# Reloading split weights through GpSimd's queue straight into the operand tiles of a 2048-frame encoder trunk

## The chip, the cores and the metric

The kernel runs on one core of one Trainium2 chip. The metric is the device time of one execution in microseconds. Three runs of the kernel before gave 2957.13, 2957.32 and 2959.49 us; the median is 2957.32 us.

## The reference

The reference is one layer of a streaming encoder for 2048 frames of width 1024, all in float32. A normed input goes through one projection (26 column blocks of 128). Its first columns feed a gated short convolution, the others an RWKV-7 recurrence of 8 heads that runs along time. Both results go through an output projection, then come a gated feed-forward block with a width-3 convolution (up to 5632 columns, down from 2816), and an embedding gated by a last projection. In outline:

```python
h = rms_norm(x, mix_norm_g);  z = h @ w_in
y = concat(short_conv_mixer(z[..., :1536]), rwkv7_mixer(z[..., 1536:]))
x = x + y @ w_out
u = causal_dwconv(rms_norm(x, ffn_norm_g) @ ffn_w_up, ffn_conv_w) + ffn_conv_b
x = x + (silu(gate) * val) @ ffn_w_down          # gate, val: the halves of u
e = rms_norm(p @ ple_w_proj, ple_norm_g)
x = x + sigmoid(rms_norm(x, ple_gate_norm_g) @ ple_w_gate) * e
return rms_norm(x, final_norm_g)
```

## The kernel before

Time is cut into four groups of 512 frames, and a product writes a 128 x 512 block of output columns by frames. Every dense product is done as three TensorE products of float32r operands: the weights and the activations are each split into a rounded part (hi) and the remainder (lo), and `mm3` adds hi·hi, hi·lo and lo·hi in one PSUM bank. One half is the unit in which weights arrive: a tile `whl` of 128 x 1024 whose left 512 columns are hi and whose right 512 are lo. It serves 12 products of 512 columns. A group needs 220 halves: 52 for the input projection and 168 for the rest (16 for `w_out`, 88 for `w_up`, 44 for `w_down`, 4 for `w_proj`, 16 for `w_gate`).

The program first runs the input projection for all four groups (`all_in`), then the dense rest for all four groups (`dense_rest`). Beside these products goes the recurrence in 16 units of 128 frames (`rwkv_unit`). A driver lets it take a step each time a product yields, so that its many small products stand between the dense ones on TensorE. TensorE's order is that of the code, since every matmul is pinned. The order on the other engines is set by a scheduler that places each instruction by estimated times. Each engine and each queue then runs its list strictly in that order.

`half` (L156 to L174) makes a half ready. The first time that a weight block is needed (the first group of the input projection and the first group of the dense rest), SP loads 256 KB of the original weights into a tile `raw`, ScalarE rounds it into hi (L153), GpSimd subtracts to get lo (L154), and SP writes the pair to a tensor `keep` in HBM (L172). Each later group takes the pair from there: SP loads 512 KB into a 128 x 1024 `raw` tile (L162), and ScalarE casts it to float32r into the operand tile (L163). There are two `raw` tiles (`WRAW`) and four operand tiles (`WHL`). A load therefore waits until the cast before the last has read its `raw` tile, and a cast waits until TensorE is done with the half four places ahead.

SP's queue carries, beside the weights: the frames of x, the mixer's results y and the embedding e (L204), the rows of x that are added after the output projection (L396, pinned in order, each into one of ten `x2` tiles), and the recurrence's loads (L562 to L567, L774, L789, L802, L809). GpSimd does, beside the lo parts of first weights: the lo part of the feed-forward activations (`lo<-th`, L154), the halo columns of the convolutions (`zb<-u_last` and `u_last<-zb`, L257 and L258), and steps of the recurrence: `s` (L613), `gd` (L573), `pb` and `pbl` (L717 to L723), two memsets of `lm` (L786), four copies `tt<-dt` (L820), and the power `gr` (L589). ScalarE evacuates and activates, and copies the state and the token operands of the recurrence.

Of the kernel before, what the change touches and what calls it, by code (L numbers as in the profile page):

```python
# [9 lines left out]
F32 = mybir.dt.float32  # L10
# [6 lines left out]
P = 128  # L17
# [11 lines left out]
RATE = 1.0  # L29
SLOW = 0.85  # L30
WRAW = 2
WHL = 4
NBUF = 6
NLD = 3
ACT = 32
# [27 lines left out]
def tile_trunk(  # L63
# [18 lines left out]
    nc = tc.nc  # L82
# [69 lines left out]
    def residual(raw, hi, lo):  # L152
        nc.scalar.copy(hi, raw)  # L153
        nc.gpsimd.tensor_tensor(out=lo, in0=raw, in1=hi.bitcast(F32), op=ALU.subtract)  # L154

    def half(pools, src, name, key):  # L156
        t = pools["w"].tile([P, 1024], F32R, tag="whl", name=f"whl{name}", bufs=WHL)
        hi, lo = t[:, 0:512], t[:, 512:1024]
        raw = pools["w"].tile([P, 1024], F32, tag="raw", name=f"raw{name}", bufs=WRAW)
        with tc.high_priority():  # L160
            if key in kept:
                nc.sync.dma_start(out=raw, in_=kept[key])  # L162
                nc.scalar.copy(t, raw)  # L163
                return hi, lo
            first = raw[:, 0:512]
            if len(src.shape) == 3:
                nc.sync.dma_start(out=first.rearrange("p (j c) -> p j c", j=2), in_=src)
            else:
                nc.sync.dma_start(out=first, in_=src)
            residual(first, hi, lo)  # L170
        keep = dram.tile([P, 1024], F32, tag=f"k{name}", name=f"k{name}")
        nc.sync.dma_start(out=keep, in_=t.bitcast(F32))  # L172
        kept[key] = keep
        return hi, lo  # L174

    kept = {}

    def weight(pools, src, name):
        return [
            half(pools, src[:, 512 * c : 512 * c + 512], f"{name}_{c}", f"{name}_{c}")  # L180
            for c in range(2)
        ]

    def quad(pools, src, mp, name):
        cols = slice(256 * mp, 256 * mp + 256)
        return [half(pools, src[:, :, cols].rearrange("j p c -> p j c"), name, name)]
# [746 lines left out]
    pools, rp = {}, {}  # L933
# [139 lines left out]
```

## Time and profile before

| | |
|---|---|
| median of three runs | 2957.32 us |
| the profiled execution | 2957.25 us |
| its span, first to last instruction | 2955.5 us |
| TensorE (PE) busy | 2784.5 us, 94% |
| weight loads into TensorE (PEld) | 2232.1 us, 76% |
| VectorE (DVE) busy | 1888.8 us, 64% |
| ScalarE (ACT) busy | 1611.2 us, 55% |
| GpSimd (POOL) busy | 763.3 us, 26% |
| DMA | 630 MB, 213 GB/s over the span |
| granted TensorE clock, mean | 0.977 |

The span is the time that the engines' rows cover; 1.75 us of the execution lie outside it. Busy shares are means over stages that differ: the input projection of the first group ends at about 196 us, that of the others at about 700 us; the dense rest of the first group goes to about 1330 us, the others follow to the end. The last unit of the recurrence ends at about 2614 us.

### The profile page before, as it was taken

Reading aid. Unit: us, or ns where it says so; the run is one execution under the profiler, and the core shown is the slowest. Engines: PE = TensorE matmul, PEld = TensorE weight load, DVE = VectorE, ACT = ScalarE, POOL = GpSimd, SP = SyncE. Lnnn points to the kernel's source line nnn. Section 1 sums busy time; section 2 is a strip of 40 time slices with the busy share of each in tenths; the row PEclk is TensorE's granted clock in tenths of the full one; section 3 lists DMA queues with packets and bytes.
Section 4 is the critical chain, followed back from the end, with each engine's and each line's share of the span. In section 5 each row is a group of like instructions: output and inputs, shape, how many; then the busy total and the mean of one; then the engine's idle time right before and its main releaser. Section 6 shows DMA issues by size and latency. Waiting matters only on the chain.

```text
span 2955.5 us, 43233 instructions
## 1 busy us (share of the span) xinstructions
PE 2784.5 (94%) x15464; PEld 2232.1 (76%) x15464; DVE 1888.8 (64%) x3039; ACT 1611.2 (55%) x2381; POOL 763.3 (26%) x1040
## 2 busy tenths in 40 slices
PE   8899999999888999988999999889999998999997
PEld 6677777778676767766788887767888876788885
DVE  4575655657586767696676677757675764544346
ACT  4345565544453434355755556667565565755555
POOL 4521010203455555550211121102111210211110
PEclk9999999999999999999999999999999999999998
DMA  8776766577776676767665655666565557666664
GB/s 295 262 262 220 225 209 220 191 228 241 239 245 237 231 251 217 249 228 258 194 193 170 188 182 176 219 204 204 177 196 170 187 184 244 203 195 197 192 195 150
DMA packets 285810, 630.02 MB, mean 213 GB/s; under 512 B 60186, under 2 KB 113690, under 8 KB 285596
## 3 DMA queue, kind: packets, MB, share of 16 engines
q1 hardware_dynamic: 229184, 578.91, 60.5%
q10 hardware_dynamic: 56412, 48.36, 5.0%
q8 instruction: 122, 2.00, 0.3%
q14 instruction: 92, 0.75, 0.1%
HBM read 467.77 MB, written 159.38 MB: 212 GB/s over the span
## 4 chain that ended last, share of the span: by engine, by line
PE 44%; DMA 20%; DVE 14%; ACT 10%; issue 8%; POOL 3%; ACTq 1%; SPq 0%; DVEq 0%; POOLq 0%
PE ps_mm L86 28%; PE ps_d L86 10%; DMA rawu<-ku 3%; DMA rawin<-kin 2%; DMA rawu<-in_w_up 2%; DMA rawin<-in_w_in 2%; DVE uf L416 2%; DMA rawo<-ko 2%; DMA x<-in_xT 2%; DVE pd L793 1%; ACT whlu L163 1%; ACT whlin L163 1%; PE o_ps L86 1%; DVE xs L797 1%; DMA dt<-xd 1%
## 5 line engine op out<-in xcount | busy, mean ns | idle before, releaser
L86 PE MATMUL ps_mm<-hi,whlu 128*128 128x512 f32 x2816 | 915.5, 399 | 11.1 <-POOL whlu L154 8.1
L86 PEld LDWEIGHTS ps_mm<-hi,whlu 128*128 128x128 f32 x2816 | 535.2, 190 | 132.7 <-POOL whlu L154 11.2
L86 PE MATMUL ps_mm<-hi,whlin 128*128 128x512 f32 x1664 | 545.4, 402 | 15.0 <-ACT whlin L153 7.0
L86 PE MATMUL ps_mm<-lo,whlu 128*128 128x512 f32 x1408 | 555.2, 394 | 1.5 <-DVE lo L216 1.5
L86 PE MATMUL ps_d<-hi,whld 128*128 128x512 f32 x1408 | 453.9, 395 | 8.2 <-DVE x L456 3.6
L163 ACT CAST whlu<-rawu 128x1024 fp32r<-128x1024 f32 x264 | 277.2, 1051 | 283.0 <-DMA rawu<-ku 194.3
L416 DVE SCALAR_TENSOR_TENSOR uf<-zb,vec,uf 128x512 f32<-128x512 f32 x352 | 291.0, 829 | 206.5 <-ACT uf L411 196.3
L86 PEld LDWEIGHTS ps_mm<-hi,whlin 128*128 128x128 f32 x1664 | 317.7, 191 | 89.8 <-ACT whlin L153 8.0
L86 PE MATMUL ps_mm<-lo,whlin 128*128 128x512 f32 x832 | 330.0, 397 | 1.3 <-DVE lo L216 1.3
L86 PEld LDWEIGHTS ps_d<-hi,whld 128*128 128x128 f32 x1408 | 264.9, 188 | 69.7 <-DVE x L456 6.0
L86 PEld LDWEIGHTS ps_mm<-lo,whlu 128*128 128x128 f32 x1408 | 268.4, 191 | 56.8 <-DVE lo L216 2.5
L86 PE MATMUL ps_d<-lo,whld 128*128 128x512 f32 x704 | 275.0, 391 | 0.0
L163 ACT CAST whlin<-rawin 128x1024 fp32r<-128x1024 f32 x156 | 163.2, 1047 | 160.2 <-DMA rawin<-kin 78.2
L256 DVE TENSOR_TENSOR zb<-ps_mm,rstd 128x512 f32<-128x512 f32 x216 | 148.1, 685 | 102.3 <-PE ps_mm L86 97.3
L456 DVE TENSOR_TENSOR x<-ps_d,x 128x512 f32<-128x512 f32 x192 | 130.9, 686 | 124.8 <-PE ps_d L86 124.1
L163 ACT CAST whld<-rawd 128x1024 fp32r<-128x1024 f32 x132 | 138.5, 1051 | 125.4 <-DMA rawd<-kd 61.6
L86 PE MATMUL ps_mm<-hi,whlo 128*128 128x512 f32 x512 | 168.4, 404 | 23.3 <-ACT whlo L163 11.4
L86 PEld LDWEIGHTS ps_mm<-lo,whlin 128*128 128x128 f32 x832 | 159.3, 191 | 36.3 <-DVE lo L216 4.3
L154 POOL TENSOR_TENSOR lo<-th,hi 128x512 fp32r<-128x512 f32 x88 | 116.7, 1327 | 219.0 <-ACT hi L153 218.4
L411 ACT ACTIVATE uf<-zb,vec 128x512 f32<-128x512 f32 x176 | 142.8, 813 | 44.2 <-DVE zb L256 42.4
L86 PE MATMUL ps_mm<-hi,whlg 128*128 128x512 f32 x512 | 165.7, 399 | 0.2 <-ACT whlg L163 0.2
L86 PEld LDWEIGHTS ps_d<-lo,whld 128*128 128x128 f32 x704 | 132.6, 188 | 25.8
(204 smaller groups left out, 4341.8 us busy)
## 6 DMA issues: line engine op xcount, KB each, us to landing
rawu<-ku SPq DMA_DIRECT2D x264, 512.0 KB, 4.2
rawin<-kin SPq DMA_DIRECT2D x156, 512.0 KB, 4.2
rawd<-kd SPq DMA_DIRECT2D x132, 512.0 KB, 4.1
ku<-whlu SPq DMA_DIRECT2D x88, 512.0 KB, 4.4
kin<-whlin SPq DMA_DIRECT2D x52, 512.0 KB, 4.9
rawo<-ko SPq DMA_DIRECT2D x48, 512.0 KB, 4.5
rawg<-kg SPq DMA_DIRECT2D x48, 512.0 KB, 4.1
rawu<-in_w_up SPq DMA_DIRECT2D x88, 256.0 KB, 3.5
```

The source lines that it names most:

```text
L86: return pin(nc.tensor.matmul(*args, **kw))
L154: nc.gpsimd.tensor_tensor(out=lo, in0=raw, in1=hi.bitcast(F32), op=ALU.subtract)
L163: nc.scalar.copy(t, raw)
L256: nc.vector.tensor_tensor(out=zb[:, 2 : G + 2], in0=ps, in1=rstd, op=ALU.mult)
L411: nc.scalar.activation(u, zb[:, 2 : G + 2], AF.Identity, bias=v("ffn_conv_b", n), scale=v("ffn_conv_w", 88 + n),)
L416: nc.vector.scalar_tensor_tensor(out=u, in0=zb[:, d : d + G], scalar=v("ffn_conv_w", 44 * d + n), in1=u, op0=ALU.mult, op1=ALU.add,)
L456: nc.vector.tensor_tensor(out=x2[m], in0=ps, in1=x2[m], op=ALU.add)
L793: tt(out=pd[:, :, :, 0:n], in0=xs[:, :, None, 0:n].broadcast_to([P, 8, 2, n]), in1=lm[:, None, i : i + 2, 0:n].broadcast_to([P, 8, 2, n]), ...
L797: nc.vector.tensor_reduce(out=xs[:, :, i : i + 2], in_=pd[:, :, :, 0:n], op=ALU.add, axis=mybir.AxisListType.X,)
```

## The change

Where a half has been kept, its load no longer goes from SP's queue into a `raw` tile with a cast by ScalarE behind it. GpSimd's queue issues one DMA from `keep` (float32) to the operand tile (float32r), and the DMA converts. The `raw` tiles are only needed for first loads and shrink from 1024 to 512 columns, and the operand tiles go from four to five.

```diff
-WHL = 4
+WHL = 5
...
     def half(pools, src, name, key):
         t = pools["w"].tile([P, 1024], F32R, tag="whl", name=f"whl{name}", bufs=WHL)
         hi, lo = t[:, 0:512], t[:, 512:1024]
-        raw = pools["w"].tile([P, 1024], F32, tag="raw", name=f"raw{name}", bufs=WRAW)
+        if key in kept:
+            with tc.high_priority():
+                nc.gpsimd.dma_start(out=t, in_=kept[key])
+            return hi, lo
+        first = pools["w"].tile([P, 512], F32, tag="raw", name=f"raw{name}", bufs=WRAW)
         with tc.high_priority():
-            if key in kept:
-                nc.sync.dma_start(out=raw, in_=kept[key])
-                nc.scalar.copy(t, raw)
-                return hi, lo
-            first = raw[:, 0:512]
```

ScalarE's list where the scores of the last unit of the recurrence are made. `whld` and `whlu` are halves of the down and up weights, `tok` the recurrence's token operand; before:

```order
L428 ACTIVATE th<-uf 128x512 [waits Pool_49]
L722 CAST pbh_21677<-pb_21674 128x512 [waits Pool_49]
L163 CAST whld_2_21786<-rawd_2_21787 128x1024 [waits DMAHW5_49,PE_49]
L163 CAST whld_2_21790<-rawd_2_21791 128x1024 [waits DMAHW6_49,PE_49]
L153 CAST hi<-th 128x512 [waits DVE_49]
L756 COPY tok_0_21749<-ps_k 128x512 [waits PE_49]
L163 CAST whld_3_21931<-rawd_3_21932 128x1024 [waits DMAHW7_49,PE_49,Activation_49]
L163 CAST whld_3_21935<-rawd_3_21936 128x1024 [waits DMAHW0_49,PE_49,Activation_49]
L756 COPY tok_1_21809<-ps_k 128x512 [waits PE_49]
```

The same place now:

```order
L427 ACTIVATE th<-uf 128x512 [waits Pool_49]
L721 CAST pbh_20797<-pb_20794 128x512 [waits Pool_49]
L153 CAST hi<-th 128x512 [waits DVE_49]
L755 COPY tok_0_20861<-ps_k 128x512 [waits PE_49]
L755 COPY tok_1_20917<-ps_k 128x512 [waits PE_49]
```

The casts, each with a wait for a DMA and for TensorE, no longer stand between the recurrence's copies.

GpSimd's list a little later in the same unit, around the memsets of `lm`; before:

```order
L723 TENSOR_TENSOR pbl_21678<-pb_21674,pbh_21677 128x512 [waits Activation_49]
L154 TENSOR_TENSOR lo<-th,hi 128x512 [waits Activation_49]
L786 MEMSET lm_21839 128x32 [waits DMAHW3_49,DMAHW2_49,DMAHW4_49,DMAHW1_49,DVE_49]
L787 MEMSET lm_21839 128x16
L257 COPY zb<-u_last 128x2 [waits Pool_49]
L258 COPY u_last<-zb 128x2 [waits DVE_49]
```

Now:

```order
L161 DMA whlu_0_21153<-ku_0_10807 128x1024 [waits DMASW7_49,PE_49]
L161 DMA whlu_1_21155<-ku_1_10814 128x1024 [waits DMASW0_49,PE_49]
L161 DMA whlu_0_21190<-ku_0_10854 128x1024 [waits DMASW1_49,PE_49]
L256 COPY zb<-u_last 128x2 [waits Pool_49]
L257 COPY u_last<-zb 128x2 [waits DVE_49]
L785 MEMSET lm_20947 128x32 [waits DMAHW6_49,DMAHW5_49,DMAHW7_49,DMAHW0_49,DVE_49]
L786 MEMSET lm_20947 128x16
L161 DMA whlu_1_21192<-ku_1_10861 128x1024 [waits DMASW2_49,PE_49]
L161 DMA whlu_0_21235<-ku_0_10909 128x1024 [waits DMASW3_49,PE_49]
```

Weight loads that wait for TensorE now stand ahead of and behind GpSimd's steps that wait for VectorE or for the recurrence's DMAs.

SP's list at the start of the last group's output projection (`rawo` are its weights, `x_3_n` the rows of x); before:

```order
L162 DMA rawo_0_23444<-ko_0_6966 128x1024
L162 DMA rawo_1_23448<-ko_1_6973 128x1024
L396 DMA x_3_2_23347<-in_xT 128x512
L396 DMA x_3_3_23390<-in_xT 128x512
L396 DMA x_3_4_23433<-in_xT 128x512
L396 DMA x_3_5_23476<-in_xT 128x512
L162 DMA rawo_0_23487<-ko_0_7015 128x1024
L162 DMA rawo_1_23491<-ko_1_7022 128x1024
```

Now:

```order
L395 DMA x_3_1_22277<-in_xT 128x512
L203 DMA p<-in_pT 128x512 x2
L395 DMA x_3_2_22351<-in_xT 128x512
L395 DMA x_3_3_22390<-in_xT 128x512
L395 DMA x_3_4_22429<-in_xT 128x512
L395 DMA x_3_5_22468<-in_xT 128x512
L395 DMA x_3_6_22507<-in_xT 128x512
```

The weight loads and the rows of x no longer share a list.

## Rows read from the trace of the kernel before

**Rows 1.** The page's part 1: busy us, share of the span, instructions.

```profile
PE 2784.5 (94%) x15464; PEld 2232.1 (76%) x15464; DVE 1888.8 (64%) x3039; ACT 1611.2 (55%) x2381; POOL 763.3 (26%) x1040
```

**Rows 2.** Busy time of each engine in stretches, granted clock, DMA share, GB/s.

```profile
196.00:700.00 504.00, 491.21 (x3016) 396.66 (x3016) 297.32 (x516) 283.55 (x412) 71.85 (x160) 0.99 0.68 217
1330.00:2895.00 1565.00, 1510.38 (x8284) 1218.32 (x8282) 978.46 (x1627) 945.78 (x1298) 261.50 (x444) 0.99 0.62 196
...
1325.00:1395.00 70.00, 62.96 (x259) 49.48 (x259) 51.93 (x89) 37.10 (x47) 7.46 (x11) 0.95 0.81 260
1890.00:1960.00 70.00, 63.36 (x273) 50.26 (x273) 51.56 (x91) 39.37 (x50) 4.55 (x9) 0.95 0.75 243
2437.00:2507.00 70.00, 61.30 (x255) 47.94 (x255) 36.67 (x55) 41.26 (x52) 4.82 (x4) 0.98 0.75 245
```

**Rows 3.** PE's waits from 1330 to 2895 us: waiter, releaser, us, times, longest.

```profile
PE ps_mm L86 <- ACT whlo L163: 11.4, 8, 3.0
PE ps_mm L86 <- DVE x L397: 8.1, 2, 4.4
...
PE ps_e L86 <- ACT hi L153: 3.6, 1, 3.6
...
PE ps_o L86 <- ACT tok L756: 2.3, 2, 1.3
...
PE ps_e L86 <- ACT e L371: 2.2, 4, 1.0
PE ps_mm L86 <- ACT hi L215: 1.7, 2, 1.0
```

**Rows 4.** PE's waits from 196 to 700 us.

```profile
PE x_ps L86 <- ACT gm L589: 4.9, 3, 2.3
PE ps_b L86 <- ACT tok L756: 2.3, 1, 2.3
PE ps_mm L86 <- ACT whlin L163: 1.9, 1, 1.9
```

**Rows 5.** Chain of waits, 2440 to 2500 us: start, us, what.

```profile
2443.61 5.34 DMA rawo<-ko
2449.04 1.06 ACT whlo L163
```

**Rows 6.** SP's queue in order of time, 2440 to 2500 us.

```profile
2456.64 20.50 SPq L162 DMA_DIRECT2D rawo<-ko  x7
2478.11 4.54 SPq L396 DMA_DIRECT2D x<-in_xT  x4
```

**Rows 7.** The casts of line 163 alone: ScalarE's busy time and count in stretches.

```profile
196.00:700.00 504.00, 159.03 (x152) 0.99 0.68 217
1330.00:2895.00 1565.00, 517.05 (x493) 0.99 0.62 196
```

**Rows 8.** Chain of waits where the recurrence is over: 16 halves on TensorE.

```profile
2614.77 43.52 PE ps_mm L86 x192
```

**Rows 9.** Line 162, SP's loads: issue ns (min/median/max), and us to landing.

```profile
L162 SPq DMA_DIRECT2D rawu<-ku x264: 319/320/692, 1385.1 to 2841.7; - x132
...
DMA to landing us min/median/max: 3.0/4.2/8.4
```

**Rows 10.** GpSimd's groups, whole span: busy us, mean ns, idle before, releasers.

```profile
L820 POOL COPY tt<-dt 32x256 f32<-32x256 f32 x64 | 27.6, 432 | 193.7 <-DMA dt<-xd 191.5
L589 POOL TENSOR_TENSOR gr<-var,neg_h 128x8 f32<-128x8 f32 x16 | 26.3, 1643 | 123.6 <-DVE var L589 122.0 <-DMA rawu<-in_w_up 1.6
...
L786 POOL MEMSET lm<- 128x32 f32 x16 | 2.6, 160 | 97.7 <-DVE lm L785 85.4 <-ACT whlin L163 7.0 <-DMA p<-in_pT 5.3
```

**Rows 11.** VectorE's copies, whole span.

```profile
L589 DVE COPY w_t<-w_ps 128x256 f32<-128x256 f32 x32 | 13.5, 420 | 13.3 <-PE w_ps L86 13.1
L589 DVE COPY tt<-x_ps 32x256 f32<-32x256 f32 x32 | 13.3, 414 | 24.4 <-PE x_ps L86 24.2
```

**Rows 12.** SP's queue on the 16 DMA engines: packets, MB, share of the span.

```profile
q1 hardware_dynamic: 229184, 578.91, 60.5%
```

## The prediction

> **What bounds the kernel now.** I read the page's busy shares first, then the busy time by stretches, then TensorE's waits in those stretches, then the chain of waits where they are longest. TensorE is busy 2784.5 of 2955.5 us [rows 1], so nothing that shortens another engine's work can give back more than its idle time and its slow clock. The change acts only where kept halves are loaded. The casts of line 163 show where that is: 152 of them between 196 and 700 us, 493 between 1330 and 2895 us [rows 7]. In these two stretches of 2069 us TensorE is idle 12.8 + 54.6 = 67.4 us, at a granted clock of 0.99 [rows 2]. The rest of the idle time lies in the first loads, the start and the tail, where neither path of a kept half runs.
>
> Within the two stretches the idle time is not spread evenly. Where all is steady, 16 halves take 43.52 us [rows 8], so TensorE uses up a half in 2.72 us. In the first 70 us of each later group's output projection it is idle 7.0, 6.6 and 8.7 us and has a clock of 0.95, 0.95 and 0.98 [rows 2]. There the chain runs through the weights' supply: a load of 5.34 us, a cast of 1.06 us, the next load [rows 5]. Two raw tiles give two halves per such round of 6.4 us, 3.2 us for one, slower than TensorE's 2.72. The queue shows the same pace: seven loads issued in 20.50 us, 2.93 us each. Then four loads of x hold SP for 4.54 us more, with weights behind them [rows 6]. The waits name it too: products of the output projection stood 11.4 us for the cast of `whlo`, and 8.1 us for rows of x that share SP's queue [rows 3]; 1.9 us went to a cast of the input weights [rows 4].
>
> **The change, part by part.**
>
> *ScalarE's casts go.* 645 casts, 676 us of ScalarE in these stretches, or 1.05 us each [rows 7]. That is beside TensorE's work, except where TensorE waits for the result. The direct waits for a cast are 11.4 + 1.9 = 13.3 us [rows 3, 4]; with the supply no longer cut into rounds of load and cast I count them gone: **-13.3 us**. ScalarE's other results that TensorE waits for, behind casts in its list, are `gm` 4.9, `tok` 2.3 and 2.3, `hi` 3.6 and 1.7, `e` 2.2 us [rows 3, 4], together 17.0 us. The least gain is none, if their inputs were late by themselves, and the most is 17.0. The two lists of ScalarE show casts directly ahead of `tok`, but not each wait had one ahead, so I take half: **-8.5 us**.
>
> *SP's queue loses its weight loads.* The loads of x then stand behind no load that waits for a raw tile. Of the 8.1 us [rows 3] I take half, since those loads also wait for a free `x2` tile: **-4 us**.
>
> *Clock.* In the three output-projection stretches a clock of 0.95, 0.95 and 0.98 over 70 us [rows 2] costs (0.05 + 0.05 + 0.02) x 70 = 8.4 us. The lower level is 1.2 GHz, half of 2.4, and idle time goes with it in these rows. About half of the idle time there goes, so I take half: **-4 us**.
>
> *GpSimd's queue gains 645 DMAs in these stretches.* No row of before shows a DMA from that queue, nor one that converts. For the issue the nearest rows are SP's 0.32 us for the same 512 KB [rows 9] below, and GpSimd's costliest short instruction, `gr` with 1.64 us [rows 10], above. I take the middle, 0.98 us. Then 645 issues are 632 us, beside 72 + 262 = 333 us of GpSimd's own work in 2069 us [rows 2]: 47% of its time, at the upper end 67%. GpSimd does not become the bound. For the landing, SP's loads show 3.0 to 8.4 us with a median of 4.2 [rows 9]; a converting one could be shorter than the median only by what queues saved, so I keep 4.2 and hold 8.4 as the upper end.
>
> *Five tiles.* A load waits until TensorE has finished the half five places ahead and has the time of four halves, 4 x 2.72 = 10.9 us. It needs 0.98 + 4.2 = 5.2 us, which leaves a cover of 5.7 us. At the upper ends it needs 1.64 + 8.4 = 10.0 us, with 0.8 us left. So the supply holds as long as GpSimd comes to the load in time. Without the fifth tile the cover would be 3.0 us.
>
> *What is queued behind the new wait.* Each load waits for TensorE at GpSimd's head, and behind it stand halo copies, `lo<-th`, and the recurrence's `s`, `lm`, `tt` and `gr`; VectorE and then TensorE wait for those. There is a load every 2.72 us or more, so an instruction that comes at a random time waits up to 1.4 us on average if GpSimd always stands at a load, and about 0.3 us (0.98 us by a share of 0.31) if loads never wait. I take 1.2 us. Four such places in each unit of the recurrence, 12 units in these stretches (three quarters of the 16 counted by `gr` [rows 10]), are 58 us of delay in that chain. TensorE has dense products to do meanwhile, so most of it is covered. I charge a quarter, a choice between none and all: **+14 us**.
>
> The Trainium skill has a rule against this change (SBUF — State Buffer, section "SBUF: two separate sides"): while VectorE runs a copy in its two-port mode, GpSimd cannot write descriptors, and a DMA issued from its queue starves. What the trace shows of VectorE's copies are 64 in the whole span, 26.8 us, and all read a PSUM tile (`w_ps`, `x_ps`) [rows 11]; the rule speaks of copies from SBUF to SBUF. If the rule held for these too, 48 copies of 0.42 us in the kept stretches would add 20 us to GpSimd in pieces far below the cover of 5.7 us, so by the rule as by the rows the sum stays the same.
>
> *First loads.* They keep their path; a narrower raw tile changes none of their instructions, and the fifth tile can help where ScalarE waited for a free one. I count zero.
>
> **Sum.** -13.3 - 8.5 - 4 - 4 + 14 = -15.8 us. The profiled execution took 2957.25 us, of which 1.75 lie outside the span, and the median of the runs is 2957.32, the same within 0.1. So 2957.25 - 15.8 = **2941 us**.
>
> **The rivals.**
>
> *GpSimd blocked (slower).* GpSimd's own waits in before: 193.7 us ahead of `tt<-dt`, 123.6 ahead of `gr`, 97.7 ahead of `lm` [rows 10], over 16 units 12.1, 7.7 and 6.1 us each. They cost nothing there, since nothing stood behind. Now weight loads stand behind. Where such a wait is longer than the cover of 5.7 us, TensorE runs dry: 6.4 + 2.0 + 0.4 = 8.8 us a unit, 106 us over 12 units if the waits stay as long. Against it: in before GpSimd came early to these places because it had nothing else to do; with loads paced by TensorE it comes later, and the scheduler places a memset by when it expects it. Half is 53 us, less the 13 us of direct waits that would still go: 2957 + 40 = **2997 us**. It decides from a wait above 5.7 us with a load next in the list.
>
> *Converting DMAs move data slowly (slower).* SP's queue moved 578.91 MB in 60.5% of the span [rows 12], 0.324 MB per us of all engines. 645 kept halves of 0.524 MB are 338 MB, 1043 us, half of the 2069 us; the DMA share there is 0.62 to 0.68 [rows 2]. If converting doubled the time the engines would need 1.14 times the stretch: 0.14 x 2069 = 290 us, **3247 us**. It decides from about 1.7 times the plain duration. Nothing in the rows speaks for it, since none shows a conversion.
>
> *Hidden anyway (no change).* The 67 us of idle time are mostly the recurrence's own; the weights' waits go, and GpSimd's new delays put back as much: within 5.9 us of 2957 (0.2%, about what a measurement of this kernel tells from no change).
>
> *The larger gain.* If all 17.0 us of waits on ScalarE, all 8.1 for x and all 8.4 of clock go, with GpSimd's delays covered: 13.3 + 17.0 + 8.1 + 8.4 = 47 us, **2910 us**.
>
> **How the numbers follow.** The forecast (2918 to 2951) has 0.40, the larger gain 0.13, hidden anyway 0.14, GpSimd blocked 0.25, slow conversion 0.08. Faster by over 0.2%: 0.53; within: 0.14; slower: 0.33. The forecast's own range is 2918 to 2951 us. With both signs held, the range goes from 2900 us, a little below the larger gain, to 3010 us, a little above half the price of a blocked GpSimd; what is left out is its full price, the slow conversion, and little below.
>
> **What would show it.** Right: no cast of line 163 on ScalarE, its busy time near 1611 - 690 = 920 us; TensorE's waits for `whlo` gone and the output-projection stretches nearly without idle time; GpSimd's busy time or its queue up by about 0.3 to 1.6 us a load; loads landing in 4 to 8 us. Wrong: TensorE's new waits end with a DMA into `whl`, and GpSimd stood at `tt`, `gr` or `lm` ahead of it (blocked), or DMA shares in the kept stretches go toward 1 (slow conversion).

## The result and the profile after

The changed kernel takes 2916.45 us (median of three, 2914.06 to 2920.32) against 2957.32 us: ratio 0.9861, 95% interval 0.9839 to 0.9884, or 41 us less. The forecast was 2941. The sign was right, the size was less than half of what came, and the forecast's own range (2918 to 2951) was missed at its lower end; the wide range held it. The profiled execution took 2920.32 us with a span of 2918.5 us.

Part 1 of the page after, as [rows 1]:

```profile
PE 2771.0 (95%) x15464; PEld 2231.7 (76%) x15464; DVE 1894.1 (65%) x3039; ACT 962.9 (33%) x1721; POOL 1109.2 (38%) x1700
```

ScalarE has 660 instructions and 648 us less. GpSimd has 660 instructions and 346 us more: the issue of each load stands there as busy time.

Busy time by stretches after (columns as in [rows 2]). The first two are the stretches of the kept halves, the other three the first 70 us of each later group's output projection, each begun 9 to 12 us ahead of its first product as in [rows 2]:

```profile
196.00:686.00 490.00, 482.62 (x3013) 390.25 (x3011) 301.12 (x521) 134.66 (x261) 151.87 (x313) 1.00 0.73 223
1315.00:2857.00 1542.00, 1505.29 (x8279) 1220.94 (x8277) 980.86 (x1624) 460.16 (x803) 518.38 (x936) 0.99 0.66 198
1309.50:1379.50 70.00, 64.04 (x300) 51.18 (x298) 50.90 (x93) 20.51 (x31) 17.62 (x32) 0.98 0.84 265
1873.50:1943.50 70.00, 64.36 (x302) 51.87 (x301) 48.04 (x88) 20.19 (x31) 14.79 (x30) 0.98 0.84 259
2421.30:2491.30 70.00, 67.97 (x289) 54.83 (x288) 35.55 (x53) 21.59 (x33) 16.40 (x28) 0.98 0.83 270
```

The two stretches are 504 - 490 = 14 and 1565 - 1542 = 23 us shorter, so all of the difference of the two profiled executions (36.9 us) lies where kept halves are loaded. TensorE's idle time in them falls from 67.4 [rows 2] to 7.4 + 36.7 = 44.1 us, by 23.3. That is not the whole of the 37: its busy time falls too, from 2001.6 [rows 2] to 482.6 + 1505.3 = 1987.9 us, by 13.7 for the same work. In the three 70 us stretches it is idle 6.0, 5.6 and 2.0 us at a clock of 0.98, where it was 7.0, 6.6 and 8.7 at 0.95, 0.95 and 0.98. The same 70 us now hold 300, 302 and 289 products instead of 259, 273 and 255, the dense ones and the recurrence's small ones counted together.

TensorE's waits after, 1315 to 2857 us, answering to [rows 3]:

```profile
PE ps_g L86 <- DVE suv L653: 7.6, 3, 3.3
PE ps_mm L86 <- DVE lo L215: 6.0, 4, 2.4
PE ps_mm L86 <- DVE x L396: 5.9, 2, 3.2
...
PE ps_mm L86 <- DMA whlo<-ko: 2.0, 1, 2.0
PE ps_e L86 <- ACT tok L755: 1.4, 1, 1.4
...
PE ps_d L86 <- DMA whld<-kd: 1.0, 2, 0.6
...
PE ps_e L86 <- ACT e L370: 0.6, 1, 0.6
PE ps_mm L86 <- ACT hi L214: 0.5, 1, 0.5
```

The same from 196 to 686 us, answering to [rows 4]:

```profile
PE ps_mm L86 <- DMA whlin<-kin: 2.4, 4, 1.2
...
PE ps_b L86 <- ACT tok L755: 1.2, 1, 1.2
...
PE x_ps L86 <- ACT gm L588: 0.3, 1, 0.3
```

No product waits for a cast. What is left of ScalarE as a releaser is small, and the head of the list is now VectorE. Over all rows of the two stretches, the waits that name ScalarE fall from 33.6 to 5.2 us, and 5.4 us of waits for loads come up. The waits that name VectorE stay: 32.6 us before, 32.4 after.

GpSimd after: two of the groups of loads, and the groups that answer to [rows 10]:

```profile
L161 POOL DMA_DIRECT2D whlu<-ku x264 | 141.8, 537 | 422.9 <-PE ps_mm L86 278.3 <-PE ps_d L86 97.9 <-PE ps_e L86 17.7
...
L819 POOL COPY tt<-dt 32x256 f32<-32x256 f32 x64 | 29.3, 458 | 68.3 <-DMA dt<-xd 65.9
L588 POOL TENSOR_TENSOR gr<-var,neg_h 128x8 f32<-128x8 f32 x16 | 27.5, 1719 | 20.0 <-DVE var L588 19.6
...
L161 POOL DMA_DIRECT2D whlo<-ko x48 | 25.7, 538 | 77.4 <-PE ps_mm L86 76.8 <-issue 0.6
...
L785 POOL MEMSET lm<- 128x32 f32 x16 | 2.5, 159 | 39.1 <-DVE lm L784 39.0
```

Issues of line 161 (ns, min/median/max) and landing, answering to [rows 9], and the queue's line, answering to [rows 12]:

```profile
L161 POOL DMA_DIRECT2D whlu<-ku x264: 527/528/612, 1360.1 to 2807.1; - x132
L161 POOL DMA_DIRECT2D whlin<-kin x156: 527/529/735, 187.1 to 689.8; - x156
...
DMA to landing us min/median/max: 3.4/4.5/11.0
```

```profile
q0 software_dynamic: 95040, 346.07, 39.4%
```

VectorE's waits show that ScalarE's list is lighter; the first of these fences is the kernel before, the second the one after (waiter, releaser, us, times, longest):

```profile
DVE uf L416 <- ACT uf L411: 196.3, 107, 5.5
```

```profile
DVE uf L415 <- ACT uf L410: 100.8, 91, 6.1
```

VectorE waited half as long for ScalarE's `uf`, while its busy time stayed (1888.8, 1894.1). ScalarE used to be the later of the two; now it is idle ahead of `uf` and waits for VectorE's `zb`. TensorE's waits that name VectorE did not fall with this (32.6, 32.4). The group of `uf` on ScalarE, before and after:

```profile
L411 ACT ACTIVATE uf<-zb,vec 128x512 f32<-128x512 f32 x176 | 142.8, 813 | 44.2 <-DVE zb L256 42.4
```

```profile
L410 ACT ACTIVATE uf<-zb,vec 128x512 f32<-128x512 f32 x176 | 143.1, 815 | 526.8 <-DVE zb L255 481.3 <-issue 44.1
```

### The profile page after: what moved, and what is told of

The parts are those of the page before. It is cut to its first block, busy times and chain, and to the rows that moved or that the text cites. A ratio compares the mean times of both kernels' runs of the same rounds, so it can differ in the third digit from the quotient of the medians.

```text
span 2918.5 us, 42094 instructions
## 1 busy us (share of the span) xinstructions
PE 2771.0 (95%) x15464; PEld 2231.7 (76%) x15464; DVE 1894.1 (65%) x3039; ACT 962.9 (33%) x1721; POOL 1109.2 (38%) x1700
## 3 DMA queue, kind: packets, MB, share of 16 engines
q0 software_dynamic: 95040, 346.07, 39.4%
## 4 chain that ended last, share of the span: by engine, by line
PE 49%; DVE 20%; DMA 16%; ACT 5%; issue 5%; POOL 3%; ACTq 1%; SPq 0%; DVEq 0%; POOLq 0%
PE ps_mm L86 33%; PE ps_d L86 11%; DVE uf L415 3%; DVE pd L792 3%; DMA rawu<-in_w_up 2%; DMA lm<-ld 2%; DVE xs L796 2%; DMA rawin<-in_w_in 2%; DMA x<-in_xT 1%; DVE zb L255 1%; DMA ld<-ltt 1%; DMA xd<-xs 1%; PE o_ps L86 1%; DMA dt<-xd 1%; DMA es<-e 1%
## 5 line engine op out<-in xcount | busy, mean ns | idle before, releaser
L415 DVE SCALAR_TENSOR_TENSOR uf<-zb,vec,uf 128x512 f32<-128x512 f32 x352 | 291.7, 831 | 111.6 <-ACT uf L410 100.8
L161 POOL DMA_DIRECT2D whlu<-ku x264 | 141.8, 537 | 422.9 <-PE ps_mm L86 278.3
L161 POOL DMA_DIRECT2D whlin<-kin x156 | 84.1, 540 | 221.0 <-PE ps_mm L86 182.8
L154 POOL TENSOR_TENSOR whlu<-rawu,whlu 128x512 fp32r<-128x512 f32 x88 | 120.0, 1364 | 109.5 <-ACT whlu L153 102.6
```

Source lines behind the costliest of these rows:

```text
L161: nc.gpsimd.dma_start(out=t, in_=kept[key])
L415: nc.vector.scalar_tensor_tensor(out=u, in0=zb[:, d : d + G], scalar=v("ffn_conv_w", 44 * d + n), in1=u, op0=ALU.mult, op1=ALU.add,)
```

## The experiments

Ratios are to the kernel before on the same chip, with 95% intervals. Times in us are medians, and "cost" or "gain" between two runs is the difference of their ratios times 2957, uncertain by some 9 us from the two intervals.

**Which part gains: the queue, the fifth tile, the cast.**

Four tiles instead of five in the changed kernel (`e1_four_tiles`):

```diff
-WHL = 5
+WHL = 4
```

> The changed kernel with four operand tiles in place of five; all else as changed. Theory A (the gain is the two-raw-tile round of load and cast that is gone, and ScalarE's freed list; depth is not used up): a load then has three halves, 8.2 us, against an issue of 0.53 us and a landing of 4.4 us in the changed kernel's trace, so it still comes in time: 2916 to 2924 us, TensorE's waits that end with a DMA into whl under 10 us. Theory B (the fifth tile carries the gain, since loads at GpSimd's head are often late): most of the 41 us come back, 2940 us or more, and such waits grow to tens of us.

Measured: 2940.80 us, 0.9938 [0.9919, 0.9957]. The fifth tile is worth 23 us when GpSimd loads. TensorE's waits for DMAs into the operand tiles were 6.1 (`whlin`), 8.9 (`whld`) and 7.1 us (`whlo`) there, and over all five kinds of weight 28.7 us in the span; in the changed kernel they are 7.1.

The kernel before with only the queue changed (`e2_load_on_gpsimd_cast_on_scalar`):

```diff
-                nc.sync.dma_start(out=raw, in_=kept[key])
+                nc.gpsimd.dma_start(out=raw, in_=kept[key])
                 nc.scalar.copy(t, raw)
```

> The kernel before with one edit: the kept halves' loads into the wide raw tiles are issued from GpSimd's queue, ScalarE still casts. SP's queue is relieved as in the change, ScalarE is not, and the round of load and cast over two raw tiles stays. Theory A: no gain, or only the part of the rows of x in SP's queue (up to 8 us): 2948 to 2962 us. Theory C (the gain is SP's queue: loads and rows of x no longer hold each other up): 2925 us or less. GpSimd blocked by waits at its head would show as a loss: above 2965 us.

Measured: 3022.74 us, 1.0218 [1.0199, 1.0238]: a loss of 64 us. Whatever SP gains by losing the loads, GpSimd's queue costs far more. GpSimd's waits in this run, and their longest:

```profile
POOL rawu L162 <- ACT whlu L163: 379.0, 178, 7.3
POOL rawin L162 <- ACT whlin L163: 282.7, 119, 6.6
```

GpSimd's list stands behind ScalarE's casts here, so two lists are tied to one another. I take that for the cause of the loss; no run tried it apart.

The changed kernel with the loads from SP, without conversion (`e3_direct_from_sp`). The tile is addressed as float32, since what `keep` holds is rounded already:

```diff
-                nc.gpsimd.dma_start(out=t, in_=kept[key])
+                nc.sync.dma_start(out=t.bitcast(F32), in_=kept[key])
```

> The changed kernel with the kept halves' loads issued from SP's queue straight into the operand tile, viewed as float32 (the bits in HBM are already rounded), so without a conversion, without ScalarE's cast and with five tiles; GpSimd has its former list. Theory A: the gain is there without GpSimd's queue: 2914 to 2925 us, the upper part if rows of x waiting for an x2 tile hold weights up in SP's list at the output projections (about 8 us at the last one). Theory D (GpSimd's queue costs something, the 14 us of the prediction): 2905 us or less. Theory C: 2940 us or more, as SP's queue is crowded again.

Measured: 2897.28 us, 0.9798 [0.9776, 0.9820], 19 us better than the changed kernel. That is what GpSimd's queue costs together with the conversion, which goes with it here; no run tried the two apart. Page, and the three output-projection stretches, of this run:

```profile
PE 2758.2 (95%) x15464; PEld 2219.1 (77%) x15464; DVE 1892.7 (65%) x3039; ACT 963.2 (33%) x1721; POOL 760.5 (26%) x1040
```

```profile
1309.60:1379.60 70.00, 64.52 (x304) 50.65 (x303) 52.55 (x93) 21.23 (x33) 7.30 (x11) 1.00 0.81 274
1863.70:1933.70 70.00, 67.12 (x319) 53.48 (x317) 48.53 (x88) 21.25 (x33) 4.06 (x8) 1.00 0.82 273
2398.90:2468.90 70.00, 67.83 (x295) 54.70 (x294) 36.35 (x53) 21.47 (x33) 3.76 (x4) 1.00 0.80 277
```

ScalarE and VectorE are as in the changed kernel and GpSimd as before; the clock in the three stretches is 1.00.

The same with four tiles (`e5_direct_from_sp_four_tiles`) and with six (`e8_six_tiles`, first loads through the staging tiles to make room):

```diff
-WHL = 5
+WHL = 4
```

```diff
-WHL = 5
+WHL = 6
...
-        first = pools["w"].tile([P, 512], F32, tag="raw", name=f"raw{name}", bufs=WRAW)
+        first = pools["tmp"].tile([P, 512], F32, tag="s", name=f"raw{name}", bufs=NLD)
```

> As e3 (direct loads from SP, no cast) with four operand tiles in place of five. In e1 the loss of the fifth tile cost 24 us with GpSimd issuing. If that was because loads at GpSimd's head are late, SP's queue, which has little else, loses less: 2900 to 2910 us. If four tiles are simply short (8.2 us for a landing of 4.2 us plus whatever holds the queue), the same 20 to 25 us are lost: 2915 to 2925 us.

> As e3 with six operand tiles; the room comes from the two raw tiles, whose first loads now take the three staging tiles that x, y, e and p use. If depth still pays after five, the kept stretches gain some 5 to 10 us over e3 and the first loads lose or gain little: 2885 to 2897 us. If sharing the staging tiles holds up the first loads, 2905 us or more.

Measured: 2916.03 us, 0.9841 [0.9818, 0.9863] with four; 2897.99 us, 0.9787 [0.9765, 0.9808] with six. On SP the fifth tile is worth 13 us, a sixth nothing that can be told. Four tiles from SP, with no casts and no wide raw tiles, are already 47 us below before: the larger part of the gain is not the depth.

Two variations of the queue: ScalarE's instead of GpSimd's (`e12_direct_from_scalar`), and two DMAs of 256 KB for one of 512 (`e11_two_dmas_a_half_on_gpsimd`):

```diff
-                nc.gpsimd.dma_start(out=t, in_=kept[key])
+                nc.scalar.dma_start(out=t.bitcast(F32), in_=kept[key])
```

```diff
-                nc.gpsimd.dma_start(out=t, in_=kept[key])
+                nc.gpsimd.dma_start(out=t[:, 0:512], in_=kept[key][:, 0:512])
+                nc.gpsimd.dma_start(out=t[:, 512:1024], in_=kept[key][:, 512:1024])
```

> The changed kernel with the kept halves loaded from ScalarE's queue (no conversion, no cast, five operand tiles). ScalarE has about 960 us of work then, and a load at the head of its list waits for a free operand tile. A, what stands behind a waiting load costs, on ScalarE more than on GpSimd, since more of the products' evacuation goes through it: 2925 to 2960 us. B, with the casts gone ScalarE's list has room, and its issue takes far less than GpSimd's 0.53 us: as from SP, 2895 to 2905 us.

> The changed kernel with each kept half loaded by two converting DMAs of 256 KB from GpSimd's queue instead of one of 512 KB: twice as many issues, the same bytes. The changed kernel has 2916 us and the same loads from SP's queue 2897, so GpSimd's queue costs 19 us. A, these are GpSimd's time for the issues (0.53 us each, 660 of them): doubled, another 19 us, 2935 us. B, they are the waits of a load for a free operand tile at the head of GpSimd's list: those do not double, 2914 to 2920 us.

Measured: 2921.57 us, 0.9879 [0.9864, 0.9893] from ScalarE, 24 us worse than from SP and much as from GpSimd. Its issue is as short as SP's (327 ns median against GpSimd's 528), so its cost is not the issue. The other reading, that work stands behind a load that waits for its tile, is argued and not shown. The trace's list of who waited for those loads does not decide it: its first rows follow, then the first two of the run from SP (`e3_direct_from_sp`), where the same names stand at the head.

```profile
  ACT uf L410: 37.6, 5
  DVE fold L781: 18.7, 3
  ACT sq L227: 11.0, 3
  PE ps_mm L86: 10.2, 9
```

```profile
  DVE fold L781: 27.7, 7
  ACT uf L410: 18.9, 1
```

Two DMAs a half: 2924.18 us, 0.9890 [0.9872, 0.9908], a cost of 9 us for 348 us more of GpSimd's time (1109.2 to 1457.2 busy). By the middle value about half of GpSimd's 19 us goes with issue time and the rest with its loads' waits for a free tile, but with 9 us of uncertainty neither part is shown.

**What the casts cost: put ScalarE's copies back beside direct loads.** In these runs a ScalarE copy into a scratch tile that nothing reads stands beside each kept half. First on GpSimd's queue (`e4_scalar_list_as_before`), then on SP's, with the copy reading the half just loaded (`e6_scalar_casts_that_wait`) or one loaded two places earlier (`e7_scalar_casts_without_wait`), all with four tiles:

```diff
                 nc.sync.dma_start(out=t.bitcast(F32), in_=kept[key])
+                scr = pools["w"].tile([P, 1024], F32R, tag="scr", name=f"scr{name}", bufs=1)
+                nc.scalar.copy(scr, seen[-3].bitcast(F32))
```

> As e1 (four tiles, converting DMAs from GpSimd), plus one ScalarE cast of 128x1024 for each kept half from the operand tile into a scratch tile that nothing reads: ScalarE's time (660 x 1.05 = 690 us) and its waits for the weights' DMAs come back, but TensorE doesn't wait for the casts. The output is the reference's. Theory A1 (the supply of weights carries the gain): within 10 us of e1, 2916 to 2932 us. Theory A2 (ScalarE's freed list carries it): 2940 to 2960 us, with TensorE's waits for tok, gm, hi and sq back.

> As e5, plus one ScalarE cast of 128x1024 for each kept half from the operand tile into a scratch tile that nothing reads: ScalarE's time and its waits for the landing are back in its list, while TensorE waits for the landing only. Output as the reference. Theory L (ScalarE's list carries the gain): 30 us or more above e5. Theory S (the supply, the round of load and cast over two raw tiles, carries it): within 10 us of e5.

> As e6, but each scratch cast reads the operand tile that was loaded two halves earlier, which has landed by then: ScalarE's 690 us are back, its waits for landings mostly not. Theory L by time (ScalarE's busy time delays the rest): near e6. Theory L by waits (an in-order list that stands at a landing): near e5, within 10 us, and e6 far above. Output as the reference.

Measured: 3014.87 us, 1.0195 [1.0173, 1.0217] on GpSimd's queue, 76 us over the run without copies (e1); 2965.23 us, 1.0014 [0.9998, 1.0029] and 2962.38 us, 1.0012 [0.9994, 1.0029] on SP's. Copies whose result nobody uses take back the whole 47 us of e5. No product needs them, and the loads are direct, so it was not the rounds of load and cast.

The traces show how the copies cost. The spans of e6 and e7 are 53 and 60 us longer than that of e5. TensorE's waits that name ScalarE go from 36.2 us over the span to 58.0 and 55.3, those for loads into operand tiles from 17.2 to 22.8 and 25.5, and those that name VectorE from 54.7 to 54.7 and 63.0. Nearly all of the rest is TensorE's busy time: 23 us more for the same 15464 products, at a lower granted clock. Span and clock, and the first part of the page, of e5 and then of e7:

```profile
core 0: 2906.5 us, clock 0.984
PE 2766.2 (95%) x15464; PEld 2220.5 (76%) x15464; DVE 1894.5 (65%) x3039; ACT 963.5 (33%) x1721; POOL 761.0 (26%) x1040
```

```profile
core 0: 2966.7 us, clock 0.975
PE 2788.8 (94%) x15464; PEld 2232.0 (75%) x15464; DVE 1898.3 (64%) x3039; ACT 1611.7 (54%) x2381; POOL 767.0 (26%) x1040
```

In e6 TensorE is busy 2789.3 us at a clock of 0.976. Over all runs the median clock is 0.983 in e5, 0.977 in e6 and 0.978 in e7; span times one less the clock then gives 16 to 19 us for the difference, an estimate. No run changed the clock by itself, so why it is lower with the copies is not shown.

My label for the last of these was wrong. Its copies did wait for landings. ScalarE's waits in that run, 1330 to 2880 us:

```profile
ACT scru L166 <- DMA whlu<-ku: 205.9, 155, 6.4
ACT scrd L166 <- DMA whld<-kd: 78.7, 64, 4.2
```

So time and waits were still one. Five tiles and copies (`e9_scalar_time_five_tiles`, first loads as in e8), and four tiles and copies of half the length (`e10_half_of_scalar_time`):

```diff
-WHL = 4
+WHL = 5
```

```diff
-                nc.scalar.copy(scr, seen[-3].bitcast(F32))
+                nc.scalar.copy(scr, seen[-3][:, 0:512].bitcast(F32))
```

> Direct loads from SP into five operand tiles (first loads land in the recurrence's staging tiles, so that a scratch tile fits), and beside each kept half a ScalarE copy of 128x1024 into the scratch tile, reading the half that was loaded two places earlier. Its result is used by nothing. The run tells ScalarE's time from the hold that the copy has on an operand tile. A, ScalarE's time in its list is what the removed casts cost: the fifth tile changes nothing of that, the loss stays near the 46 us that it had with four tiles, so 2940 to 2957 us. B, the copy costs because a tile comes free only when ScalarE has read it: the fifth tile gives one more half (2.7 us) of slack, most of the loss goes, 2900 to 2920 us.

> As the run with four tiles and unawaited ScalarE copies (2962 us against 2916 without them), but each copy has 512 columns instead of 1024, so about half the time of ScalarE and the same number of instructions. A, the loss goes by ScalarE's busy time: half of 46 us, 2939 us. B, it goes by the number of instructions in the list (their order and semaphores): 2955 to 2962 us. C, it goes by the square, as a wait behind a longer instruction in a fuller list does: a quarter, about 2928 us.

Measured: 2958.09 us, 1.0009 [0.9996, 1.0022] with five tiles, 62 us over e3, so the hold on a tile is not the cause (B falls), and beside the copies the fifth tile is worth next to nothing. The traces agree: SP's loads waited for TensorE's `ps_mm` as long in e7 as in e5 (1071.8 and 1066.2 us), and no row in e7 that has them wait for a copy has more than 4.5 us. The copies of half the length took 2953.04 us, 0.9988 [0.9971, 1.0004], a cost of 43 us against 50 at full length. Busy time alone does not set it.

Then the two apart: copies of 128x8, with all the waits and little of the time (`e15_waits_without_time_aligned`; ScalarE is busy 101 us more than in e5, where the full copies make it 648), and operations of 128x1024 that hang on no load (`e14_time_without_waits`):

```diff
-                nc.scalar.copy(scr, seen[-3].bitcast(F32))
+                nc.scalar.copy(scr[:, 0:8], seen[-3][:, 0:8].bitcast(F32))
```

```diff
+                if last[1] < 3:
+                    last[1] += 1
+                    nc.scalar.activation(scr, scr, AF.Copy, scale=last[0].bitcast(F32))
```

> The run with 128x8 copies again, but with a scratch tile of 128x1024 of which only 8 columns are written, so that every other tile lies where it lay with the copies of 1024 columns. In the first such run the scratch tile took 32 bytes a partition and every dense product of the run, those of the first group too, took 233.3 ns where all other runs show 226.7 to 229; over some 10,500 dense products that is about 59 us, so it said nothing on the waits. A, the loss of the copies is ScalarE's waits for landings: 2945 to 2962 us. B, it is ScalarE's time: 2912 to 2925 us, as without copies (2916). Against B speaks that copies of 512 columns lost 37 of 46 us.

> Direct loads from SP into four operand tiles, and beside a kept half (567 of 645) a ScalarE operation of 128x1024 on a scratch tile that hangs on no load: it takes its scale from the result that ScalarE itself made last in the program, at most three of them for one such result, so they stand right behind that result in its list and wait for nothing. About 600 us of ScalarE's time without waits for landings, in pieces of up to three in a row. A, the loss is the waits for landings in ScalarE's list: 2916 to 2930 us. B, it is ScalarE's time: 2945 to 2965 us.

Measured: 2933.67 us, 0.9923 [0.9905, 0.9941] for the waits, 2938.48 us, 0.9929 [0.9912, 0.9945] for the time. Each costs about half: 24 and 26 us over e5, together the 50 of e7. Neither side of the expectation held: as far as these two runs go, both causes are there. Half the time and all the waits make 24 + 13 = 37 by this, where e10 measured 43, within the intervals. The two runs' ScalarE groups from 1330 to 2880 us (busy, mean ns of one, idle ahead), waits first:

```profile
L166 ACT CAST scru<-whlu 128x8 fp32r<-128x8 f32 x228 | 44.5, 195 | 364.6 <-DMA whlu<-ku 364.3
...
L166 ACT CAST scrd<-whld 128x8 fp32r<-128x8 f32 x102 | 19.9, 196 | 133.5 <-DMA whld<-kd 133.2
```

```profile
L102 ACT ACTIVATE scr<-scr,hi 128x1024 f32<-128x1024 f32 x219 | 251.7, 1149 | 4.9 <-ACT hi L92 0.3
L102 ACT ACTIVATE scr<-scr,uf 128x1024 f32<-128x1024 f32 x118 | 135.8, 1151 | 78.1 <-DVE uf L438 72.7 <-DVE pd L815 3.6
```

The second is not a perfect control: its 567 operations come in pieces of up to three in a row, which the casts did not, and some hang on VectorE through the result that they take their scale from.

**A run that said nothing on its question.** The waits were first tried with a scratch tile of 32 bytes a partition (`e13_waits_without_time`), and then a pad of that size was put into e5 without copies (`e16_layout_32_bytes`):

```diff
-                scr = pools["w"].tile([P, 1024], F32R, tag="scr", name=f"scr{name}", bufs=1)
-                nc.scalar.copy(scr, seen[-3].bitcast(F32))
+                scr = pools["w"].tile([P, 8], F32R, tag="scr", name=f"scr{name}", bufs=1)
+                nc.scalar.copy(scr, seen[-3][:, 0:8].bitcast(F32))
```

```diff
+    pad = pools["w"].tile([P, 8], F32, tag="pad", name="pad", bufs=1)
+    nc.vector.memset(pad, 0.0)
```

> Direct loads from SP into four operand tiles, and beside each kept half a ScalarE copy of 128x8 (instead of 128x1024 or 128x512) out of the half that was loaded two places earlier, into a scratch tile that nothing reads. The copies stand in ScalarE's list where a landing is expected, as the longer ones did, and wait there for DMAs, but take almost no time. 2916 us without copies, 2962 with 1024 columns, 2953 with 512. A, the loss is that ScalarE's list waits for landings: most of it stays, 2940 to 2955 us. B, it is ScalarE's time: it goes, 2914 to 2925 us.

> Direct loads from SP into four operand tiles, no copies, and one tile of 128x8 (32 bytes a partition) ahead of the activation tiles, written once and read by nothing. If the place of the activation tiles alone makes a product longer, every dense product takes 233 ns instead of 227 and the time is 2916 + 55 to 65 = 2970 to 2980 us; if not, 2916.

Measured: 2970.81 us, 1.0035 [1.0021, 1.0049], and 2912.70 us, 0.9847 [0.9828, 0.9866]. In the first, TensorE's products were longer. Where the recurrence is over and TensorE is never idle, 259 of them fall in 60 us, against 266 in e5 (e13 first, then e5):

```profile
2700.00:2760.00 60.00, 60.00 (x259) 48.16 (x258) 24.24 (x36) 13.13 (x36) 7.33 (x18) 1.00 0.59 188
```

```profile
2700.00:2760.00 60.00, 60.00 (x266) 49.71 (x265) 26.52 (x39) 11.10 (x16) 7.74 (x20) 1.00 0.63 195
```

The clock is 1.00 in both. The kernels before and after have 267 each in these 60 us, so nothing of the kind is in the change's own gain. In e15, with the same copies and a scratch tile of another size, it is gone, so it goes with that tile and not with the copies; a pad of the same size at the head of the pool did not bring it back. Where the tiles came to lie was not looked at, and the cause stays open.

## Why the prediction was too small

**The sum as the runs have it.** From before to four tiles loaded directly by SP: -47 us. The fifth tile: -13. GpSimd's queue and the conversion instead of SP's queue: +19. Together -41, as measured; the three are steps of one path, so they add up by themselves. The forecast had -21.8 for the casts' waits and ScalarE's results, -4 for x, -4 for the clock, nothing for the tile, +14 for GpSimd.

**ScalarE: the step that failed.** The prediction held that the casts lie beside TensorE's work except where TensorE waits, and it priced them by the waits that name ScalarE alone: 13.3 for the casts and at most 17.0, half of it taken, for `gm`, `tok`, `hi` and `e`. The copies put back cost 50. The waits were not far off. In the two stretches those that name ScalarE fell by 28.4 us, 13.0 of the 17.0 among them, and 5.4 came back as waits for loads; the copies put back brought 22 and 19. What the sum left out is TensorE's busy time for the same products: 23 us more with the copies, at a granted clock of 0.976 and 0.975 instead of 0.984, and 13.7 us less in the two stretches of the change. The bound at the head of the prediction held, since 37 us is less than 67.4 of idle time and some 21 at a clock of 0.99. But the clock was then counted in three stretches of 70 us only, and apart from the casts.

A step further back there was no better price. VectorE's waits for ScalarE's `uf` fell from 196.3 to 100.8 us in the change and went from 104.4 in e5 to 163.7 in e6, while TensorE's waits that name VectorE stayed both times (32.6 and 32.4; 54.7 and 54.7).

By e14 and e15, half of the cost is the casts' time, and half is that each cast stood in ScalarE's list waiting for its load, with other results behind it. The prediction asked that question of GpSimd's new waits, and not of ScalarE's old ones.

**Casts' direct waits, -13.3.** They went: 11.4 and 1.9 us became waits for loads of 2.0 (`whlo`), 1.0 (`whld`) and 2.4 us (`whlin`). But the reason given, rounds of load and cast paced by two raw tiles, is not borne out as a cost of its own: e6 and e7 have no raw tile in the path and no gain.

**SP's queue, -4.** The waits for rows of x fell from 8.1 [rows 3] to 5.9 us, so 2 of the 4. The term by itself was not tried; e3, with all loads still on SP, is the fastest, so it is not needed for any of the gain.

**Clock, -4.** 0.95, 0.95, 0.98 became 0.98 three times: (0.03 + 0.03) x 70 = 4.2 us. It held in these stretches, and e3 with 1.00 shows what was left. But the clock rose elsewhere too: 0.99 to 1.00 over the 490 us from 196 on is some 5 us that the prediction gave nothing for. Over the whole span the clock was 0.977 and is 0.979 in the two profiled executions, 7 us by span times one less the clock, an estimate; the median of the three runs after is 0.981.

**GpSimd's queue, +14.** Measured 19, the conversion included. That the two lie so near is luck in part. The issue took 0.53 us, not 0.98. GpSimd stood idle 1.6 us ahead of a load (422.9 us ahead of 264 in the largest group), but the delay of what comes behind, taken as 1.2 us, stands in no row, nor does the quarter of it that was charged. For the way that the prediction gave, over VectorE to TensorE, speaks that TensorE's waits that name VectorE are 75.5 us over the span of the changed kernel and 60.4 in e3.

**Five tiles.** The prediction gave the cover (5.7 us against 3.0) and priced it at nothing. It was worth 23 us on GpSimd's queue and 13 on SP's, and TensorE's waits for loads were 28.7 us without it and 7.1 with it on GpSimd's queue, 17.2 and 7.9 on SP's. Landings had a median of 4.5 and a longest of 11.0 us, beyond the 8.4 that was held as the upper end.

**The rivals.** GpSimd blocked: its waits at `tt`, `gr` and `lm` fell from 193.7, 123.6 and 97.7 us [rows 10] to 68.3, 20.0 and 39.1, so the argument against it held, that GpSimd comes later to places where it waited for want of work. Slow conversion: 346.07 MB in 39.4% of 2918.5 us are 0.301 MB per us against 0.324, 7% slower, far from the factor 1.7 at which it would decide. As for the rule of the Trainium skill (SBUF — State Buffer, section "SBUF: two separate sides"), by which VectorE's two-port copies starve GpSimd's descriptors: VectorE's copies read PSUM [rows 11], and with VectorE busy 65% of the span, the longest issue took 0.735 us against a median of 0.53, so nothing of the kind shows here. The larger gain (2910) was the nearest case, but its 47 us leave out the fifth tile, and they hold GpSimd's delays for covered, which cost 19 with the conversion.

**What would show it.** No cast of kept halves, no wait for `whlo` of any size, landings of 4.5 us and an issue inside the bounds: right. ScalarE at 920 us: it was 962.9. Output projections nearly without idle time: true of the third only (2.0 us).

## What to carry to other kernels

The waits that name an engine price only TensorE's idle time. Work taken off that engine was worth more than twice as much here, since TensorE's busy time for the same products fell with it, at a higher granted clock: compare busy time and clock over the whole span, and not only the waits or the stretches where the clock is lowest. Ask of each list, old or new, what stands in it behind an instruction that waits for a load. In this kernel, loads that wait for a free tile did best in a queue that no arithmetic shares: from SP they were 19 us better than from GpSimd with conversion and 24 better than from ScalarE, with the same tiles. The version from SP with five tiles, no cast and no conversion, is the best of both kernels and all runs (2897.28 us, 0.9798; six tiles the same): where the stored bits are already rounded, nothing has to convert them.

## What the runs showed of the hardware that was not expected

GpSimd's issue takes the same for 256 KB (530 ns least, e11) as for 512 KB (527), so halves of a load double its price; for 512 KB SP's and ScalarE's take 319 (e3) and 321 (e12). A converting load landed in 4.5 us, hardly later than a plain one from SP (4.2 before, 4.1 in e3). And in e13, with a scratch tile of 32 bytes, products were some 3% longer at full clock (259 against 266 in 60 us), in e16 with a pad of that size they were not, and the runs did not pin down the reason.
